# A hybrid decoder layer: mixer in source order, block inversion with one block per partition, TensorE output transposes, operands moved by 32 bytes

## The chip, the cores and the metric

The kernel runs on one core of one Trainium2 chip. The metric is the time of one execution in microseconds of device time; the smaller the better.

## What is computed

One decoder layer over 256 tokens of width 2048, all in float32: a SwiGLU feed-forward half step (FFN1), a mixer, a second feed-forward half step (FFN2), and a last RMSNorm. The mixer projects the normalised input with one weight `w_in` and feeds eight retention heads and eight gated DeltaNet heads; both join in one output projection `w_out`. The part that the change rewrites is the triangular solve of the DeltaNet heads.

```python
x = x + 0.5 * _swiglu(_rmsnorm(x, norm_ffn1_w), ffn1_w_gate, ffn1_w_up, ffn1_w_down)      # D_FF = 5632
x = x + _mixer(_rmsnorm(x, norm_mix_w), ...)
x = x + 0.5 * _swiglu(_rmsnorm(x, norm_ffn2_w), ffn2_w_gate, ffn2_w_up, ffn2_w_down)
# in _gated_delta, per head and chunk of the sequence:
m = where(strict, einsum(k_beta, k) * decay, 0.0);  a = m + eye
sol = triangular_solve(a, [v * beta, k_beta * exp(gc)], lower=True, unit_diagonal=True)
```

## The kernel before

Every large product is computed in three matmuls (`triple`, L149 to L151): weights and activations are split into a high and a low float32r part, and hi*hi, lo*hi and hi*lo are added up in PSUM. The activation tile (128x128: `xh`/`xl` for the normalised input, `hh`/`hl` for the hidden layer of an FFN, `mh`/`ml` and the like for the mixer's output) is the stationary operand, the weight (128x512) the moving one. A product of a 512-column block over 16 row tiles and two token tiles is 96 matmuls. The weights stream in as 512 KB pieces of two row tiles: SP issues the DMA into `raw` (four buffers), ScalarE makes `whi` (L135), VectorE `wlo` (L136), four buffers each; a piece is prepared three pieces before TensorE uses it. A piece feeds twelve matmuls.

The mixer runs 16 products with `w_in`, four for each of q, k, v and gate of both kinds of heads in two groups of four heads, then four with `w_out`. The small work of the heads is cut into generators in two lanes, `chains` and `side`. After each *unit* of a product (one `triple`, three matmuls) `advance` lets each lane go on until it says how many units to wait (`yield n`). That is the order of the source. In the FFNs the engines PE, DVE and Activation issue in that order (`tc.manual_schedule`); in the mixer before, the framework's scheduler orders all engines by its own estimate of times.

In `delta_chain` (L721) each group of four heads makes eight 128x128 unit triangular matrices `Nt`. Their inverse `Y` starts from the 32-row diagonal blocks (L795 to L829): the blocks are gathered in `Nd` by GpSimd, written to DRAM (`nd`), and spread by DMA from there so that each partition has the rows that it needs (`spread`, L806: four DMAs of 128 KB for every four columns j, eight times for each group, issued by GpSimd). For each of 31 columns VectorE makes one multiply and one subtract over 8 x (31-j) elements (L825, L826):

```python
V.tensor_tensor(yn[:, :, :w], nr[:, j - j0, :, j + 1:], Yd[:, :, j:j + 1].broadcast_to([P, NM, w]), ALU.mult)
V.tensor_tensor(Yd[:, :, j + 1:], Yd[:, :, j + 1:], yn[:, :, :w], ALU.subtract)
```

ScalarE and GpSimd copy the blocks into `Y` (L829), VectorE transposes them into `X` (L832), and two doubling levels of 64-column matmuls follow, four to a PSUM buffer (`quad`, L785, L791), each followed by a VectorE operation on the buffer. Seven calls of `four` (L709, L713; four matmuls of 128 columns) give the outputs. The DeltaNet and retention outputs are transposed on VectorE in 32x32 blocks (`vector_transposed`, L246, L254, into `mt`) and split into the stationary operands of `w_out` (`mixed_chain`, L919).

Where a tile lies: pools are stacked, and the pools of an FFN and `gd` of the mixer begin where the pools open at that time end. Worked out from the tiles' sizes (each padded to 32 bytes), `xh` and `xl` begin at an odd multiple of 32 bytes; `hh` and `hl` of FFN1 and the tiles of `gd` begin at a multiple of 64, since the pool `par` (2912 bytes) is open below them; for FFN2 `par` is closed, and `hh` and `hl` are back at an odd multiple of 32. The weight buffers are at an odd multiple of 32 all the time.

Of the kernel before, what the change touches and what calls it, by code (L numbers as in the profile page):

```python
# [31 lines left out]
LEAD = 3  # L32
NLEV = 7
# [3 lines left out]
JC = 4  # L37
# [14 lines left out]
C_EYE = C_SL + P  # L52
C_LEV = C_EYE + B0
# [5 lines left out]
def _constants():  # L59
# [12 lines left out]
    c[:, C_EYE:C_EYE + B0] = r % B0 == np.arange(B0)  # L72
# [15 lines left out]
def hybrid_layer(ctx: ExitStack, tc: tile.TileContext, a: dict, out: bass.AP):  # L88
# [10 lines left out]
    mx = ctx.enter_context(tc.tile_pool(name="mx", bufs=4, space=PSUM))  # L99
# [209 lines left out]
    def ffn(idx, factor, after, lead=None):  # L309
# [159 lines left out]
    with tc.tile_pool(name="gd", bufs=1) as gd:  # L469
        def mixed_out(o, b, xt=None):  # L470
            for t in range(NT):
# [4 lines left out]
        env = dict(x_left=x_left, ident=ident, mx=mx, product=product, product_units=product_units, power=power,  # L476
                   vector_transposed=vector_transposed, split=split,
# [34 lines left out]
def mixer(tc, a, gd, env):  # L512
    nc = tc.nc
    V, S, G, PE = nc.vector, nc.scalar, nc.gpsimd, nc.tensor
    x_left, ident, mx, power = (env[k] for k in ("x_left", "ident", "mx", "power"))
    vector_transposed, split = env["vector_transposed"], env["split"]
    product, product_units, weight_piece = (env[k] for k in ("product", "product_units", "weight_piece"))
# [6 lines left out]
    with ExitStack() as ctx:  # L524
# [61 lines left out]
        def gates_chain():  # L586
# [3 lines left out]
            yield 8  # L590
# [3 lines left out]
            weight_piece(src, KD, 2 * NH, both=(wab[:, :, 0, :], wab[:, :, 1, :]))  # L594
            abt = mx.tile([P, 512], F32, name="mx")
# [45 lines left out]
        def rotary_chain():  # L641
# [17 lines left out]
            for _ in range(2):  # L659
# [4 lines left out]
                for part in parts:  # L664
                    for tx in (th.bitcast(F32), tl):
                        V.scalar_tensor_tensor(ang, tx, -part, ang, ALU.mult, ALU.add)
# [5 lines left out]
            return  # L672
            yield
# [5 lines left out]
        def conv_chain(src, ct0, dst):  # L679

            y = pb.tile([P, GH, T], F32, name="y", bufs=1)
            for i in range(0, GH, 2):
# [11 lines left out]
                yield 2  # L694
            S.activation(dst, y, AF.Silu)
# [25 lines left out]
        def delta_chain(gi, kq, vT):  # L721

            hs = gi * GH
# [362 lines left out]
```

## Time and profile before

| | us |
|---|---|
| median of 3 runs (lowest, highest) | 2015.61 (2011.86, 2018.29) |
| the profiled execution | 2015.32 |
| its span, first to last instruction | 2013.5 |
| TensorE busy | 1974.1 (98%) |
| VectorE busy | 1315.8 (65%) |
| ScalarE busy | 890.9 (44%) |
| GpSimd busy | 86.9 (4%) |

The span is what the rows below divide up; the profiled execution is 1.8 us longer than its span. Busy time of TensorE counts modelled ends of pipelined matmuls, so it says that TensorE rarely waits, not that it runs at its peak. How fast it runs is read from the starts of its matmuls.

### The profile page before, as it was taken

How to read it: one execution, taken by the hardware profiler on the slowest of the kernel's cores; microseconds unless marked ns; L12 is line 12 of the kernel's file. 1: busy time of each engine (PE TensorE's matmuls, PEld its weight loads, DVE VectorE, ACT ScalarE, POOL GpSimd, SP SyncE). 2: the span in 40 equal slices, each digit the busy share in tenths (PEclk: the TensorE clock that was granted, in tenths of full speed). 3: DMA queues.
4: the chain of work that ended last, by engine and by line, in shares of the span. 5: the costliest groups of instructions: out<-in, count | busy, mean ns of one | idle time of the engine just before them, and what ended most of it. 6: DMA issues, size and time to landing. Idle time of an engine off the chain costs nothing.

```text
span 2013.5 us, 23688 instructions
## 1 busy us (share of the span) xinstructions
PE 1974.1 (98%) x8804; PEld 1617.5 (80%) x8804; DVE 1315.8 (65%) x1878; ACT 890.9 (44%) x1076; POOL 86.9 (4%) x121
## 2 busy tenths in 40 slices
PE   9999999999999999998998999999999999999998
PEld 7888888888888888866877778888888888888886
DVE  6776664457666766564896697766676554667654
ACT  6434443343444446633643344444444434444443
POOL 0000000000000000220132100000000000000000
PEclk9999999999999999998998999999999999999999
DMA  8655655565565566797468555666665556655564
GB/s 302 202 185 188 208 190 188 188 191 186 188 208 189 183 188 181 153 207 161 145 180 200 124 158 184 215 192 194 194 193 187 200 195 192 195 192 188 184 208 142
DMA packets 197604, 379.91 MB, mean 189 GB/s; under 512 B 15280, under 2 KB 15920, under 8 KB 197360
## 3 DMA queue, kind: packets, MB, share of 16 engines
q1 hardware_dynamic: 193888, 368.40, 59.5%
q0 software_dynamic: 3168, 8.65, 1.7%
q8 instruction: 69, 1.13, 0.2%
q10 hardware_dynamic: 432, 1.34, 0.2%
q14 instruction: 47, 0.39, 0.1%
HBM read 375.98 MB, written 2.36 MB: 188 GB/s over the span
## 4 chain that ended last, share of the span: by engine, by line
PE 85%; DVE 5%; DMA 4%; issue 4%; POOL 1%; ACT 1%; DVEq 0%; POOLq 0%; ACTq 0%
PE acc L149 28%; PE acc L151 27%; PE acc L150 27%; DMA nr<-nd 2%; DVE wlo L136 2%; DMA raw<-in_w_in_dram 1%; PE mx L791 1%; DVE mt L254 0%; PE mx L713 0%; DMA nd<-Nd 0%; DVE yn L825 0%; ACT whi L135 0%; DVE Yd L826 0%; POOL nr L810 0%; DVE ht L254 0%
## 5 line engine op out<-in xcount | busy, mean ns | idle before, releaser
L136 DVE TENSOR_TENSOR wlo<-raw,whi 128x1024 fp32r<-128x1024 f32 (+1 forms) x689 | 838.7, 1225 | 557.4 <-ACT whi L135 554.4
L135 ACT CAST whi<-raw 128x1024 fp32r<-128x1024 f32 (+1 forms) x689 | 719.3, 1050 | 859.4 <-PE acc L151 738.6
L149 PE MATMUL acc<-whi,xh 128*128 128x512 f32 x1920 | 760.5, 396 | 1.4 <-DVE xl L269 1.3
L150 PE MATMUL acc<-wlo,xh 128*128 128x512 f32 x1920 | 751.5, 391 | 6.7 <-DVE wlo L136 6.7
L151 PE MATMUL acc<-whi,xl 128*128 128x512 f32 x1920 | 750.8, 391 | 0.0
L150 PEld LDWEIGHTS acc<-wlo,xh 128*128 128x128 f32 x1920 | 362.1, 189 | 81.7 <-DVE wlo L136 10.8
L149 PEld LDWEIGHTS acc<-whi,xh 128*128 128x128 f32 x1920 | 362.1, 189 | 75.7 <-ACT whi L135 3.4
L151 PEld LDWEIGHTS acc<-whi,xl 128*128 128x128 f32 x1920 | 361.8, 188 | 75.4
L149 PE MATMUL acc<-whi,hh 128*128 128x512 f32 x704 | 276.5, 393 | 0.0
L150 PE MATMUL acc<-wlo,hh 128*128 128x512 f32 x704 | 276.5, 393 | 0.0
L151 PE MATMUL acc<-whi,hl 128*128 128x512 f32 x704 | 276.5, 393 | 0.0
L254 DVE STREAM_TRANSPOSE ht<-h 32x256 f32<-32x256 f32 x352 | 153.3, 436 | 5.3
L150 PEld LDWEIGHTS acc<-wlo,hh 128*128 128x128 f32 x704 | 132.4, 188 | 30.0
L151 PEld LDWEIGHTS acc<-whi,hl 128*128 128x128 f32 x704 | 132.4, 188 | 29.9
L149 PEld LDWEIGHTS acc<-whi,hh 128*128 128x128 f32 x704 | 132.4, 188 | 29.8
L141 ACT CAST hh<-ht 128x512 fp32r<-128x512 f32 x44 | 27.2, 618 | 121.3 <-DVE ht L254 121.3
L298 POOL TENSOR_TENSOR rfac<-rms,cexpn 128x2 f32<-128x2 f32 (+1 forms) x5 | 3.2, 642 | 866.0 <-DVE rms L304 866.0
L142 DVE TENSOR_TENSOR hl<-ht,hh 128x512 fp32r<-128x512 f32 x44 | 30.3, 688 | 14.5 <-ACT hh L141 14.4
L345 ACT ACTIVATE sg<-acc,rfac 128x512 f32<-128x512 f32 x44 | 29.9, 689 | 20.2 <-PE acc L151 17.4
L149 PE MATMUL acc<-whi,mh 128*128 128x512 f32 x96 | 38.1, 396 | 0.0
L151 PE MATMUL acc<-whi,ml 128*128 128x512 f32 x96 | 38.1, 396 | 0.0
L150 PE MATMUL acc<-wlo,mh 128*128 128x512 f32 x96 | 38.0, 396 | 0.0
(205 smaller groups left out, 843.8 us busy)
## 6 DMA issues: line engine op xcount, KB each, us to landing
raw<-in_ffn_w_up_dram SPq DMA_DIRECT2D x176, 512.0 KB, 4.4
raw<-in_ffn_w_down_dram SPq DMA_DIRECT2D x176, 512.0 KB, 4.4
raw<-in_ffn_w_gate_dram SPq DMA_DIRECT2D x175, 512.0 KB, 4.4
raw<-in_w_in_dram SPq DMA_DIRECT2D x128, 512.0 KB, 4.8
raw<-in_w_out_dram SPq DMA_DIRECT2D x32, 512.0 KB, 4.3
nr<-nd POOLq DMA_DIRECT2D x64, 128.0 KB, 7.7
x<-in_x_dram SPq DMA_DIRECT2D x4, 512.0 KB, 6.8
out_dram<-x SPq DMA_DIRECT2D x8, 256.0 KB, 2.4
```

The lines of the kernel that those rows point to most:

```text
L135: S.copy(hi, raw)
L136: V.tensor_tensor(lo, raw, hi.bitcast(F32), ALU.subtract)
L141: S.copy(hi, src)
L142: V.tensor_tensor(lo, src, hi.bitcast(F32), ALU.subtract)
L149: PE.matmul(o, lhsT=sh, rhs=hi, start=first, stop=False)
L150: PE.matmul(o, lhsT=sh, rhs=lo, start=False, stop=False)
L151: PE.matmul(o, lhsT=sl, rhs=hi, start=False, stop=last)
L254: V.transpose(dv[q:q + Q, :, :, r:r + Q], sv[r:r + Q, :, :, q:q + Q])
L298: G.tensor_tensor(dst, src, cexp[e][:, 0:1].broadcast_to([P, w]), ALU.pow)
L345: S.activation(sg[:, t, :], g[t], AF.Silu, scale=rf[:, t:t + 1])
L791: PE.matmul(pt[:m, i, :], lhsT=lhsT, rhs=rhs, start=True, stop=True)
```

## The change

- The mixer joins the FFNs: PE, DVE and Activation issue in source order (`tc.manual_schedule`), and the waits of the generators (`yield`) are set anew. Tiles are made late: `kq` and `vT` when the convolution needs them, a `pe` buffer (three now) only when the third last was read (`until`), `y` under a lock (`hold`), retention's `kT` and `v` when the group before is done. The query of retention's first group is projected earlier (in `mixer_plan` too); the rotary tables start with the first product.
- The blocks are inverted one per partition: 8 matrices x 4 blocks = 32 blocks, four copies of each (RS = 4), copy r holding the rows r, r+4, ... of the result. `nd` is written in 128-byte runs, loaded once as four DMAs of 128 KB (`Ub`); the recursion works on (31-j) x (j//4+1) elements; the result goes through DRAM a second time (`yd`, four DMAs, then `Yd`), in 128-byte runs. `spread` and its 64 DMAs are gone. `Y`'s copies are on ScalarE and VectorE.
- The quads have a PSUM pool of one buffer (`qd`), the other small work three (`mx`) in place of four.
- The outputs are transposed by TensorE through `mx`, and split from PSUM.
- A 32-byte tile `pad` is put first into FFN1's pool and into `gd`. With the constant `C_EYE` gone, `par` is 128 bytes smaller.

```diff
-    mx = ctx.enter_context(tc.tile_pool(name="mx", bufs=4, space=PSUM))
+    mx = ctx.enter_context(tc.tile_pool(name="mx", bufs=3, space=PSUM))
+    qd = ctx.enter_context(tc.tile_pool(name="qd", bufs=1, space=PSUM))
...
+            if idx == 1:
+
+                hp.tile([P, PAD], F32, name="pad")
...
-        for c0 in ([O_GK, O_GQ, O_GV, O_GZ, O_GZ + half] + [o + half for o in (O_GK, O_GQ, O_GV)]
-                   + [o + g for g in (0, half) for o in (O_RQ, O_RK, O_RV, O_RG)]):
+        for c0 in ([O_GK, O_GQ, O_GV, O_GZ, O_GZ + half, O_RQ] + [o + half for o in (O_GK, O_GQ, O_GV)]
+                   + [O_RK, O_RV, O_RG] + [o + half for o in (O_RQ, O_RK, O_RV, O_RG)]):
...
-    with tc.tile_pool(name="gd", bufs=1) as gd:
+    with tc.manual_schedule(engines={E.PE, E.DVE, E.Activation}), tc.tile_pool(name="gd", bufs=1) as gd:
+        gd.tile([P, PAD], F32, name="pad")
...
-        def finish_chains():
-            while chains or side:
+        def until(done):
+
+            while not done():
                 advance()
 
-        rf, gs = [], {}
+        held = set()
+
+        def hold(name):
+            while name in held:
+                yield 1
+            held.add(name)
+
+        rf, pes, read, PES = [], [], set(), 3
 
         def evacuated(col, dst=None, func=AF.Copy):
             ps, units = product_units(x_left, w_in, rows, col)
             run(units)
             if dst is None:
-                dst = pb.tile([P, NT, NB], F32, name="pe")
+
+                until(lambda: len(pes) < PES or id(pes[-PES]) in read)
+                dst = pb.tile([P, NT, NB], F32, name="pe", bufs=PES)
+                pes.append(dst)
             for t in range(NT):
                 S.activation(dst[:, t, :], ps[t], func, scale=rf[0][:, t:t + 1])
             return dst
...
         def conv_chain(src, ct0, dst):
+            yield from hold("y")
             y = pb.tile([P, GH, T], F32, name="y", bufs=1)
+            dst = dst()
...
-                yield 2
-            S.activation(dst, y, AF.Silu)
+                if i + 2 == GH:
+                    read.add(id(src))
+                    S.activation(dst, y, AF.Silu)
+                    held.discard("y")
+                yield 6
...
-            X = gd.tile([P, GH * NT, P], F32, name="X")
-            Y = gd.tile([P, GH * NT, P], F32, name="Y")
...
-                pt = mx.tile([P, 4, HALF], F32, name="mx")
+                pt = qd.tile([P, 4, HALF], F32, name="qd")
...
-            NM = GH * NT
+
+            NM, BS, RS = GH * NT, P // B0, P // (GH * NT * (P // B0))
+            BP = NM * BS
             Nd = gd.tile([P, NM, B0], F32, name="Nd", tag="st")
             for q in range(0, P, B0):
                 G.tensor_copy(Nd[q:q + B0], Ntf[q:q + B0, :, q:q + B0])
-            nd = dr.tile([P, NM * B0], F32, name="nd")
-            nc.gpsimd.dma_start(nd, Nd.rearrange("p m c -> p (m c)"))
-            ndv = nd.rearrange("(b j) x -> b (j x)", j=B0)
+            nd = dr.tile([NM, P, B0], F32, name="nd")
+            nc.gpsimd.dma_start(nd.rearrange("m p c -> p m c"), Nd)
+            Ub = gd.tile([P, B0, B0], F32, name="Ub", tag="X")
+            Yb = gd.tile([P, B0 // RS, B0], F32, name="Yb")
+            G.memset(Yb, 0.0)
+            for r in range(RS):
+                G.memset(Yb[r * BP:(r + 1) * BP].rearrange("p a c -> p (a c)")[:, r::B0 + RS], 1.0)
+            for r in range(RS):
+                nc.gpsimd.dma_start(Ub[r * BP:(r + 1) * BP].rearrange("p j c -> p (j c)"),
+                                    nd.rearrange("m (b j) c -> (m b) (j c)", j=B0))
+            Y = gd.tile([P, NM, P], F32, name="Y")
             G.memset(Y, 0.0)
-            Yd = gd.tile([P, NM, B0], F32, name="Yd")
-            G.tensor_copy(Yd, C(C_EYE, B0).unsqueeze(1).broadcast_to([P, NM, B0]))
-
-            def spread(j0):
-                nr = gd.tile([P, JC, NM, B0], F32, name="nr", bufs=2)
-                n = JC * NM * B0
-                for b in range(P // B0):
-                    nc.gpsimd.dma_start(nr[b * B0:(b + 1) * B0].rearrange("p j m c -> p (j m c)"),
-                                        ndv[b, j0 * NM * B0:j0 * NM * B0 + n].partition_broadcast(B0))
-                return nr
-
-
-            yield 4
-            nrs = [spread(0)]
-            yield 14
-            for j0 in range(0, B0, JC):
-                if j0 + JC < B0:
-                    nrs.append(spread(j0 + JC))
-                nr = nrs[j0 // JC]
-                for j in range(j0, min(j0 + JC, B0 - 1)):
-                    w = B0 - 1 - j
-                    yn = gd.tile([P, NM, B0], F32, name="yn")
-                    V.tensor_tensor(yn[:, :, :w], nr[:, j - j0, :, j + 1:], Yd[:, :, j:j + 1].broadcast_to([P, NM, w]), ALU.mult)
-                    V.tensor_tensor(Yd[:, :, j + 1:], Yd[:, :, j + 1:], yn[:, :, :w], ALU.subtract)
-                    yield 2
+
+
+            yield 28
+            for j in range(B0 - 1):
+                w, n = B0 - 1 - j, j // RS + 1
+                yn = gd.tile([P, 3 * B0], F32, name="yn")
+                yv = yn[:, :n * w].rearrange("p (i c) -> p i c", c=w)
+                V.tensor_tensor(yv, Ub[:, j:j + 1, j + 1:].broadcast_to([P, n, w]), Yb[:, :n, j:j + 1].broadcast_to([P, n, w]), ALU.mult)
+                V.tensor_tensor(Yb[:, :n, j + 1:], Yb[:, :n, j + 1:], yv, ALU.subtract)
+                yield 1
+            yd = dr.tile([NM, P, B0], F32, name="yd")
+            for r in range(RS):
+                nc.gpsimd.dma_start(yd.rearrange("m (b a r) c -> r (m b) a c", b=BS, r=RS)[r], Yb[r * BP:(r + 1) * BP])
+            Yd = gd.tile([P, NM, B0], F32, name="Yd", tag="st")
+            nc.gpsimd.dma_start(Yd, yd.rearrange("m p c -> p m c"))
+            yield 32
             for i, q in enumerate(range(0, P, B0)):
-                (S.copy, G.tensor_copy)[i % 2](Y[q:q + B0, :, q:q + B0], Yd[q:q + B0])
-            yield 10
+                (S.copy, V.tensor_copy)[i % 2](Y[q:q + B0, :, q:q + B0], Yd[q:q + B0])
+            yield 2
+            X = gd.tile([P, NM, P], F32, name="X")
...
+            def kq(part):
+                if part == 0:
+                    ins["kq"] = gd.tile([P, GH, 2, T], F32, name="kq")
+                return ins["kq"][:, :, part, :]
+
+            def vT():
+                ins["vT"] = gd.tile([P, GH, T], F32, name="vT", tag="ml")
+                return ins["vT"]
+
+            chains.append(conv_chain(evacuated(O_GK + cs), 8 + hs, partial(kq, 0)))
+            chains.append(conv_chain(evacuated(O_GQ + cs), hs, partial(kq, 1)))
+            chains.append(conv_chain(evacuated(O_GV + cs), 16 + hs, vT))
+            chains.append(delta_chain(gi, ins))
...
-            mt = gd.tile([P, GH, T], F32, name="mt", tag="dec")
-            for piece in vector_transposed(mt, src):
-                yield 2
-                piece()
             for i in range(0, GH, 2):
-                yield 1
-                split(parts[0][:, i:i + 2], parts[1][:, i:i + 2], mt[:, i:i + 2])
+                yield 3
+                pt = mx.tile([P, 2, T], F32, name="mx")
+                for j in range(2):
+                    for t in range(NT):
+                        PE.transpose(pt[:, j, t * P:(t + 1) * P], src[:, t, (i + j) * P:(i + j + 1) * P], ident)
+                split(parts[0][:, i:i + 2], parts[1][:, i:i + 2], pt)
+            read.add(id(src))
...
         def rotated_chain(src, dst):
...
-            yield 6
+            read.add(id(src))
+            yield 8
             for t in range(NT):
                 V.tensor_tensor(r[:, t, :, 0, :], r[:, t, :, 0, :], t2[:, t, :, 0, :], ALU.subtract)
                 V.tensor_tensor(r[:, t, :, 1, :], r[:, t, :, 1, :], t2[:, t, :, 1, :], ALU.add)
-            yield 5
+            yield 6
...
+        def rotated(col, name):
+            src = evacuated(col)
+            dst = rt.tile([P, GH, T], F32, name=name)
+            side.append(rotated_chain(src, dst))
+            return dst
+
+        def retention_products(gi, qT):
             hs, cs = gi * GH, gi * GW
-            q = evacuated(O_RQ + cs)
-            qT = rt.tile([P, GH, T], F32, name="rqT")
-            side.append(rotated_chain(q, qT))
-            k = evacuated(O_RK + cs)
-            kT = rt.tile([P, GH, T], F32, name="rkT")
-            side.append(rotated_chain(k, kT))
+            kT = rotated(O_RK + cs, "rkT")
+            until(lambda: len(done) == gi)
...
+        done = []
         chains.append(gates_chain())
+        side.append(rotary_chain())
         delta_products(0)
         delta_gate(0)
         delta_gate(1)
-        side.append(rotary_chain())
+        q0 = rotated(O_RQ, "rqT")
         delta_products(1)
-        r0 = retention_products(0)
+        r0 = retention_products(0, q0)
         chains.append(mixed_chain(NH, gates[0], ["kq"]))
         chains.append(mixed_chain(NH + GH, gates[1], ["X", "Y"]))
         chains.append(mixed_chain(0, r0, ["At", "Nt"]))
-        r1 = retention_products(1)
+        r1 = retention_products(1, rotated(O_RQ + GW, "rqT"))
...
-        finish_chains()
+        until(lambda: not chains and not side)
```

## Rows read from the trace of the kernel before

**Rows 1.** One line of the code: FFN1's gate activations, 4 blocks of 2 products.

```profile
L345 ACT ACTIVATE sg<-acc,rfac x8: 689/690/691, 117.4 to 248.6; 128x512 f32<-128x512 f32 x8
```

**Rows 2.** First and last matmul starts of the w_in stage, in TensorE's timeline.

```profile
735.20 0.39 PE L149 MATMUL acc<-whi,xh 128*128 128x512 f32 x1
...
1195.48 0.39 PE L149 MATMUL acc<-whi,m 128*128 128x512 f32 x1
```

**Rows 3.** Same timeline: small matmuls between two units (start, length).

```profile
937.89 0.33 PE L791 MATMUL mx<-X,Nt 128*128 128x64 f32 x2
...
938.81 0.33 PE L791 MATMUL mx<-X,Nt 128*128 128x64 f32 x2
...
822.14 0.60 PE L701 MATMUL mx<-ident,kq 128*128 128x128 f32 x4
...
823.97 0.60 PE L701 MATMUL mx<-ident,kq 128*128 128x128 f32 x4
...
955.10 1.05 PE L713 MATMUL mx<-vh,Y 128*128 128x128 f32 x8
...
957.37 1.05 PE L713 MATMUL mx<-w,kd 128*128 128x128 f32 x8
```

**Rows 4.** Stretches: busy us of each engine (instructions), granted clock, DMA share, GB/s.

```profile
730.00:1210.00 480.00, 453.92 (x2157) 369.51 (x2156) 334.87 (x644) 222.00 (x322) 84.16 (x113) 0.98 0.68 169
...
860.00:870.00 10.00, 8.02 (x28) 6.55 (x29) 9.65 (x19) 3.36 (x4) 1.93 (x4) 0.83 0.63 136
910.00:920.00 10.00, 2.97 (x11) 2.25 (x10) 5.66 (x11) 3.94 (x5) 1.18 (x3) 0.66 1.03 186
...
1090.00:1100.00 10.00, 6.01 (x22) 5.34 (x22) 5.22 (x11) 2.11 (x4) 1.65 (x2) 0.53 0.65 136
```

**Rows 5.** Waits of the w_in stage: who for whom, us, times, longest.

```profile
DVE yn L825 <- DMA nr<-nd: 24.9, 6, 9.2
...
PE mx L791 <- DVE X L832: 13.0, 2, 7.0
```

**Rows 6.** Weight DMAs at 740 to 750, then 895 to 910: KB, us to landing.

```profile
raw<-in_w_in_dram SPq DMA_DIRECT2D x4, 512.0 KB, 4.2
...
raw<-in_w_in_dram SPq DMA_DIRECT2D x4, 512.0 KB, 10.8
```

**Rows 7.** DMA issues of nd and of one narrow weight, then nr's range.

```profile
nd<-Nd POOLq DMA_DIRECT2D x2, 128.0 KB, 4.5
raw<-in_w_in_dram SPq DMA_DIRECT2D x1, 128.0 KB, 5.2
...
DMA to landing us min/median/max: 3.7/7.7/10.7
```

**Rows 8.** One line: additions after four down products, FFN1, then FFN2.

```profile
L365 DVE SCALAR_TENSOR_TENSOR x<-acc,x x8: 679/682/684, 303.5 to 405.3; 128x512 f32<-128x512 f32 x8
...
L365 DVE SCALAR_TENSOR_TENSOR x<-acc,x x8: 681/682/684, 1579.8 to 1678.4; 128x512 f32<-128x512 f32 x8
```

**Rows 9.** Stretches inside the w_out products and FFN2's down products.

```profile
1200.00:1250.00 50.00, 50.00 (x215) 40.22 (x214) 37.78 (x54) 22.35 (x30) 0.00 (x0) 1.00 0.57 194
1600.00:1650.00 50.00, 50.00 (x223) 41.39 (x222) 25.03 (x23) 19.42 (x19) 0.00 (x0) 1.00 0.57 195
```

**Rows 10.** VectorE's timeline at the first recursion: idle time before, in brackets.

```profile
859.92 0.42 DVE L825 TENSOR_TENSOR yn<-nr,Yd 128x248 f32<-128x248 f32 x1 [9.15 <-DMA nr<-nd]
```

**Rows 11.** TensorE's timeline just after it.

```profile
861.98 0.80 PE L150 MATMUL acc<-wlo,xh 128*128 128x512 f32 x1 [2.45 <-DVE wlo L136]
```

**Rows 12.** Lines of the stage by form: busy us, mean ns, idle before.

```profile
L136 DVE TENSOR_TENSOR wlo<-raw,whi 128x1024 fp32r<-128x1024 f32 x143 | 176.2, 1236 | 62.9 <-ACT whi L135 62.2
...
L254 DVE STREAM_TRANSPOSE mt<-pe 32x256 f32<-32x256 f32 x32 | 14.0, 436 | 0.6
...
L843 DVE TENSOR_TENSOR Pm<-mx,cst 128x256 f32<-128x256 f32 x8 | 3.4, 425 | 19.6 <-PE mx L791 19.6
...
L825 DVE TENSOR_TENSOR yn<-nr,Yd 128x40 f32<-128x40 f32 x2 | 0.4, 204 | 0.1
```

More of the change, by code (lines that the diff above doesn't have):

```diff
@@ L32 @@
 LEAD = 3
+PAD = 8
 NLEV = 7
@@ L36 @@
 B0 = 1 << LEV0
-JC = 4
 RET_W = NH * HD
@@ L51 @@
 C_SL = C_U + P
-C_EYE = C_SL + P
-C_LEV = C_EYE + B0
+C_LEV = C_SL + P
 C_INVF = C_LEV + (NLEV - LEV0) * HALF
@@ L474, in mixed_out @@
             later.extend(norm_block(ssqs[2], 2, b, xt))
-        env = dict(x_left=x_left, ident=ident, mx=mx, product=product, product_units=product_units, power=power,
-                   vector_transposed=vector_transposed, split=split,
+        env = dict(x_left=x_left, ident=ident, mx=mx, qd=qd, product=product, product_units=product_units, power=power,
+                   split=split,
                    weight_piece=weight_piece, do_later=do_later, mixed_out=mixed_out,
@@ L514, in mixer @@
     V, S, G, PE = nc.vector, nc.scalar, nc.gpsimd, nc.tensor
-    x_left, ident, mx, power = (env[k] for k in ("x_left", "ident", "mx", "power"))
-    vector_transposed, split = env["vector_transposed"], env["split"]
-    product, product_units, weight_piece = (env[k] for k in ("product", "product_units", "weight_piece"))
+    x_left, ident, mx, qd, power = (env[k] for k in ("x_left", "ident", "mx", "qd", "power"))
+    product, product_units, weight_piece, split = (env[k] for k in ("product", "product_units", "weight_piece", "split"))
     w_in = a["w_in"][0]
@@ L664, in rotary_chain @@
                 for part in parts:
+                    yield 4
                     for tx in (th.bitcast(F32), tl):
@@ L671, in rotary_chain @@
             S.activation(cosT, ang, AF.Sin)
-            return
-            yield
         def bc(ap, n=P):
@@ L719, in mixer, with delta_chain @@
         gates, mixed = {}, []
-        def delta_chain(gi, kq, vT):
+        def delta_chain(gi, ins):
             hs = gi * GH
+            kq, vT = ins["kq"], ins["vT"]
             kT, qT = kq[:, :, 0, :], kq[:, :, 1, :]
@@ L908, in delta_products @@
             hs, cs = gi * GH, gi * GW
-            k = evacuated(O_GK + cs)
-            kq = gd.tile([P, GH, 2, T], F32, name="kq")
-            chains.append(conv_chain(k, 8 + hs, kq[:, :, 0, :]))
-            q = evacuated(O_GQ + cs)
-            chains.append(conv_chain(q, hs, kq[:, :, 1, :]))
-            v = evacuated(O_GV + cs)
-            vT = gd.tile([P, GH, T], F32, name="vT", tag="ml")
-            chains.append(conv_chain(v, 16 + hs, vT))
-            chains.append(delta_chain(gi, kq, vT))
+            ins = {}
+            def kq(part):
[9 more added lines that the diff above has]
+            chains.append(delta_chain(gi, ins))
         def mixed_chain(r0, src, tags):
@@ L929, in mixed_chain @@
             mixed.append((r0, *parts))
-            mt = gd.tile([P, GH, T], F32, name="mt", tag="dec")
-            for piece in vector_transposed(mt, src):
-                yield 2
-                piece()
             for i in range(0, GH, 2):
-                yield 1
-                split(parts[0][:, i:i + 2], parts[1][:, i:i + 2], mt[:, i:i + 2])
+                yield 3
[5 more added lines that the diff above has]
+            read.add(id(src))
         def rotated_chain(src, dst):
+            yield from hold("y")
             r = pb.tile([P, NT, GH, 2, 64], F32, name="y", bufs=1)
@@ L948, in rotated_chain @@
                 V.tensor_tensor(r[:, t], sv[:, t], cb, ALU.mult)
-            yield 6
+            read.add(id(src))
+            yield 8
             for t in range(NT):
@@ L960, in rotated_chain @@
                 S.copy(dst[:, i:i + 2, :], pt)
+                if i + 2 == GH:
+                    held.discard("y")
                 yield 1
@@ L989, in retention_chain @@
                 S.copy(o[:, t], op[t])
+            done.append(hs)
             yield 3
@@ L1013, in retention_chain @@
             gate.append(None)
-        def retention_products(gi):
-            hs, cs = gi * GH, gi * GW
-            q = evacuated(O_RQ + cs)
-            qT = rt.tile([P, GH, T], F32, name="rqT")
-            side.append(rotated_chain(q, qT))
-            k = evacuated(O_RK + cs)
-            kT = rt.tile([P, GH, T], F32, name="rkT")
-            side.append(rotated_chain(k, kT))
+        def rotated(col, name):
[4 more added lines that the diff above has]
+        def retention_products(gi, qT):
+            hs, cs = gi * GH, gi * GW
+            kT = rotated(O_RK + cs, "rkT")
+            until(lambda: len(done) == gi)
             v = evacuated(O_RV + cs, rt.tile([P, NT, NB], F32, name="rv"))
```

2 lines of the change are left out of this document (removed).

## The prediction

> **What bounds the kernel now.** I read the windows first, then the starts of the large matmuls, then the waits and the DMA rows inside the mixer. Four blocks of FFN1 put their first and last gate activations at 117.4 and 248.6 us [rows 1]; less the 0.7 us by which the second of a pair follows the first, six products took 130.5 us, so a product of 96 matmuls takes 21.75 us and a matmul 226.6 ns, with nothing in between. In the FFNs TensorE is the bound and has no gaps to give. Its rate, however, is not the same everywhere. The additions that close FFN1's four down products span 101.8 us, those of FFN2's 98.6 us [rows 8], for the same 432 matmuls between them: 3.2 us, or 7.4 ns for each. In w_out 50 us hold 215 matmuls, in FFN2's down product 223, both at a granted clock of 1.00 [rows 9]: the mixer's output operands run at the slower rate too.
>
> The mixer is the place that loses time. Its 16 w_in products go from 735.20 to 1195.48 us [rows 2]: 460.3 us, against 16 x 21.75 = 348.0. The excess is 112.3 us. Part of it is the heads' own work on TensorE, which stays. A unit of three large matmuls with one quad matmul takes 0.92 us instead of 0.68: 0.24 each. Two units with four transposes take 1.83 instead of 1.36: 0.47. Two units with a `four` take 2.27: 0.91 for 512 columns [rows 3]. From the code there are 64 quad matmuls (15.4 us), 32 sets of transposes (15.0), 14 `four` (12.7), and 8 x 512 + 8 x 384 + 2 x 1536 columns in decay products, scores and retention outputs (about 18 at the same price per column). The gates' product and the cumulated decays I estimate at 7. Together 68. The other 44 us are waits, and lost clock.
>
> Where are they? The whole stretch has 480 - 453.9 = 26.1 us of idle TensorE; three stretches of 10 us hold 13.0 of it (2.0, 7.0 and 4.0), and in just these the granted clock falls to 0.83, 0.66 and 0.53 [rows 4], which means a third, two thirds and nearly all of them at 1.2 GHz instead of 2.4. Each fall comes with TensorE having stood idle for microseconds. Half of the busy time at the low level is lost: 1.7 + 1.5 + 2.8 = 6 us. All three lie where `spread` runs. VectorE waits 24.9 us for `nr`, and TensorE 13.0 us, in two waits, for `X`, that is for the end of the recursion [rows 5]. The `nr` transfers also slow the weights: a 512 KB piece lands in 10.8 us there, in 4.2 before the recursion [rows 6]. A piece is used up in 12 x 0.2266 = 2.72 us, so three pieces of lead are 8.2 us, and 10.8 is too late. I put 5 us of short weight waits to this: 13 + 6 + 5 = 24 of the 44 us belong to `spread`. The other 20 are spread over hand-offs between TensorE and VectorE.
>
> **The change, part by part.**
>
> *The 32 bytes.* FFN1's `hh`/`hl` and the tiles of `gd` move to an odd multiple of 32 bytes, where `xh` and FFN2's `hh` lie already, which run at 226.6 ns. 2 x (4 x 144 + 4 x 120)/2 = 1056 matmuls of FFN1's down products and 384 of w_out gain 7.4 ns each: 7.8 + 2.8 = 10.6 us. All of them are on the path, as nothing interrupts them. The bounds are 0 (the address is not the cause) and 10.6. I take 10.6: address is all that differs between the two FFNs' down products.
> [...]
>
> *`spread` goes.* 64 DMAs of 128 KB become, in each group, one of 128 KB out (`nd`), four in (`Ub`), four quarter-size ones out (`yd`) and one in (`Yd`). The steady interference has no source any more: -24 us. What takes its place are two trips to DRAM, each awaited once. First trip: GpSimd's four gathers, its memsets and the issues of the DMAs, for which I estimate 6 us; `nd`, 4.5 us; a landing of `Ub` at `nr`'s median 7.7 [rows 7]: 18 us, against 28 units x 0.68 = 19.0 us of cover. With both landings at `nr`'s longest, 10.7, it is 27 us and VectorE stands 8 us too long. Its price is known: before, VectorE stood 9.15 us [rows 10] and TensorE then 2.45 [rows 11], so some 6.7 us are free. Second trip: 3 us of issues by estimate, 7.7 and 4.5, 15 us, or 24 with two landings of 10.7, against 32 units = 21.8 us. I take 0 for both trips, with 0 to 16 us as bounds, 16 being what the same hand-off cost before: 13 us of waiting for `X` and 3 of clock.
> The 128-byte runs are new. A row near it: the narrow weight piece, 128 KB in runs of 64 bytes, landed in 5.2 us, `nd` in runs of 1 KB in 4.5 [rows 7]. So I let short runs cost nothing more.
> The Trainium skill (DMA: Bandwidth & Descriptors, Specifications) asks for 512 bytes at least, below which the engines read, modify and write; by that rule the trips would be the third case below. The row of the 64-byte runs does not show it.
>
> *The recursion on VectorE.* An operation of 248 elements takes 0.42 us, one of 40 takes 0.204 [rows 10, 12], or 0.16 + 1.02 ns per element. The elements fall from 3968 to 1560 in 31 pairs: 18.2 us become 13.3 for each group. The 64 transposes into `mt` go, at 0.436: 28 us. VectorE is not on the path, so both are worth only the cover they add. In the 31 units of a recursion, 21 us, VectorE now has 13.3 + 8 x 1.24 for splits [rows 12] = 23 us to do; the 6.7 us above take up the 2.
>
> *Transposes on TensorE.* 16 x 2 = 32 transposes, 8 sets of 0.47 [rows 3]: +3.8 us, on the path.
>
> *Source order, and fewer buffers.* Every engine now stands at the head of its own queue. The second group's quads end in the second unit of a weight piece, behind a split of 1.24 us on VectorE (I counted the yields); the single quad buffer then keeps TensorE waiting some 0.5 us for each of eight quads: 4 us. The first group's end at the last unit of a piece, ahead of the next split, and cost nothing. Three `mx` buffers under six sets of transposes in a row at the end of the mixer, where seven steps have no product under them, and the norm factors that VectorE awaits from GpSimd, I keep at the old price. VectorE is less full there: of the 20 us of hand-offs I drop 8. Left are 20 - 8 + 4 = 16 us; the bounds are 4 (every hand-off covered) and 53 (below). Earlier rotary tables and late-made tiles move work into products with free VectorE time: 0. Where that cover is gone, one split late is 1.2 us.
>
> **Sum,** against the profiled execution of 2015.3 us, which is 0.3 below the median of the three runs: 2015.3 - 10.6 - 44 + 16 + 3.8 = 1980.5. I predict 1980 us.
>
> **The rivals.**
>
> *Few waits are left.* The hand-offs shrink to 4 us. For it: the first recursion's products lose only a split here and there. Against it: the old kernel, with four buffers, did not get there. 1980 - 12 = 1968.
>
> *The trips are late.* The wait for `nr` turns into one for `Ub` and `Yd`: 16 us again, 1996. For it: in-order VectorE blocks the splits behind it, and 27 us is more than 19. Against it: only an eighth of the bytes is loaded.
>
> *The shift does nothing.* Then the two rates come from something else that differs between FFN1 and FFN2: 1980 + 10.6 = 1991. Against it stands the w_out stretch, which shares only the address with FFN1.
>
> *In-order queues become the bound (slower).* TensorE, in source order, reaches each of 16 quads and 14 `four` results while VectorE still has a whole split and the operation itself ahead: 1.24 + 0.43 = 1.67 us [rows 12], or 1.9 with the longer operation behind a `four`. 16 x 1.67 + 14 x 1.9 = 53 us, of which 4 are counted: 2029. It decides from 35 / 30 = 1.2 us per hand-off. For it: there is one quad buffer where there were four. Against it: the first group's quads end ahead of the split.
>
> **How the numbers follow.** The forecast (1971 to 1987) has 0.50; few waits (1964 to 1971) 0.21; late trips (1987 to 2000) 0.13; a shift without effect 0.06; the slower case 0.05; the same queues at half that price, about no change, 0.02; still faster than 1964, 0.03. The range 1965 to 2000 leaves out about 0.12. A change below 0.3%, 6 us, can't be told from none: faster 0.93, same 0.02, slower 0.05.
>
> **What would show it.** The FFN1 down products should take 98.6 us where they took 101.8, and w_out 223 matmuls in 50 us. The w_in stage should fall from 460 to some 436 us, with granted clock 1.00 in nearly all of it and weights landing in 4 to 5 us throughout. VectorE's waits for `nr` should be replaced by a wait for `Ub` under 6 us; TensorE's waits for `X` should be gone, and small waits for `Pm` or `Y` in the second group should be there. The prediction is wrong if `Ub` or `Yd` land more than 25 us after their source, if the address changes no rate, or if TensorE's idle time in the mixer stays above 25 us.

## The result, and the profile after

The changed kernel takes 2026.11 us (median of 4 runs, 2025.33 to 2027.28), the kernel before 2015.92 in the same comparison: a ratio of 1.0053, 95% interval 1.0036 to 1.0071. It is slower by half a per cent, where 1980 us and 1.8% faster were forecast. The profiled execution took 2025.3 us, with a span of 2023.6 where it was 2013.5.

Outside the mixer's first stage the large matmuls reached the expected rate. The additions behind FFN1's four down products now span 98.5 us, as FFN2's do [rows 8], and a stretch of 50 us in w_out holds 222 matmuls where it held 215 [rows 9]:

```profile
L367 DVE SCALAR_TENSOR_TENSOR x<-acc,x x8: 680/682/684, 302.8 to 401.3; 128x512 f32<-128x512 f32 x8
```

The stretches of the changed kernel (busy us of PE, PEld, DVE, ACT, POOL with their instructions, granted clock, DMA share, GB/s):

```profile
727.00:1200.00 473.00, 439.96 (x2100) 355.92 (x2098) 306.58 (x609) 211.17 (x311) 57.00 (x71) 0.97 0.62 150
770.00:780.00 10.00, 7.55 (x26) 5.57 (x24) 5.90 (x10) 6.63 (x8) 0.00 (x0) 0.83 0.32 90
...
820.00:830.00 10.00, 7.75 (x25) 5.95 (x26) 6.89 (x19) 4.17 (x5) 2.58 (x2) 0.66 0.66 129
860.00:960.00 100.00, 98.25 (x479) 79.35 (x478) 62.32 (x118) 40.13 (x45) 9.47 (x16) 1.00 0.81 169
1000.00:1010.00 10.00, 3.95 (x14) 2.42 (x14) 7.76 (x14) 3.98 (x6) 0.00 (x0) 0.89 0.51 158
1010.00:1020.00 10.00, 3.23 (x7) 2.35 (x8) 7.60 (x16) 5.19 (x7) 4.79 (x5) 0.50 0.20 56
1215.00:1265.00 50.00, 50.00 (x222) 41.42 (x221) 32.10 (x42) 21.17 (x27) 0.00 (x0) 1.00 0.55 179
```

The 100 us of the first recursion, 860 to 960, are nearly full and at full clock; there the old kernel had two of its three low-clock stretches [rows 4]. But the w_in stage as a whole grew from 460.3 us [rows 2] to 472.6, between these two matmuls of TensorE's timeline:

```profile
727.39 0.39 PE L148 MATMUL acc<-whi,xh 128*128 128x512 f32 x1
...
1199.95 0.47 PE L148 MATMUL acc<-whi,m 128*128 128x512 f32 x1
```

The holes are elsewhere now: 1000 to 1020 us is two thirds empty, and the clock falls to 0.50 in it. TensorE's idle time from 727 to 1200 us is 33.0 us (473.00 - 439.96), above the 25 that the prediction named as a sign of being wrong. The waits of TensorE and ScalarE from 727 to 1300 us (engine, line, waited for: us, times, longest) name the places:

```profile
PE mx L754 <- DVE gu L750: 16.5, 2, 11.5
PE acc L149 <- DVE wlo L135: 7.3, 7, 1.5
PE mx L987 <- DVE y L980: 4.0, 4, 2.1
PE qd L808 <- DVE Pm L862: 3.1, 2, 2.4
PE acc L148 <- ACT whi L134: 2.4, 2, 1.7
...
ACT y L705 <- DVE y L707: 31.3, 12, 3.6
```

TensorE's wait for `X` [rows 5] is gone but for 0.2 us, and VectorE waits for no DMA of the inversion. In its place TensorE stands 16.5 us, in two waits, at the decay products (L754), and ScalarE stands twelve times in the convolution (L705). One stretch of the three engines' timelines shows both (start, length, instruction, and in brackets the idle time before it with what ended it), ScalarE first, then VectorE, then TensorE:

```profile
994.52 0.47 ACT L705 ACTIVATE y<-mx,cw 128x256 f32<-128x256 f32 x1 [3.03 <-DVE y L707]
996.64 1.06 ACT L711 ACTIVATE kq<-y 128x1024 f32<-128x1024 f32 x1 [1.65 <-DVE y L707]
997.61 1.03 ACT L134 CAST whi<-raw 128x1024 fp32r<-128x1024 f32 x1
...
995.03 1.52 DVE L707 SCALAR_TENSOR_TENSOR y<-mx,cw,y 128x255 f32<-128x255 f32 x3 [0.54 <-ACT y L705]
998.67 1.23 DVE L135 TENSOR_TENSOR wlo<-raw,whi 128x1024 fp32r<-128x1024 f32 x1 [2.12 <-ACT whi L134]
...
1015.76 1.65 DVE L750 TENSOR_SCALAR gu<-cst,g 128x128 fp32r<-128x128 f32 x8
...
1004.90 0.40 PE L150 MATMUL acc<-whi,xl 128*128 128x512 f32 x1
1016.77 1.49 PE L754 MATMUL mx<-gu,slr 128*128 128x512 f32 x2 [11.47 <-DVE gu L750]
```

ScalarE waits 3.03 us for VectorE's part of the convolution; the high split (`whi`) stands behind that; VectorE then waits 2.12 us for the split. So the two engines work in turn, weights are prepared late, and when TensorE reaches the decay product at 1005 us, VectorE needs 11 us more to come to that place in its list.

### The profile page after: what moved, and what is told of

Same layout as the page of the kernel before. It is cut to its first block, busy times and chain, and to the rows that moved or that the text cites. A ratio compares the mean times of both kernels' runs of the same rounds, so it can differ in the third digit from the quotient of the medians.

```text
span 2023.6 us, 23594 instructions
## 1 busy us (share of the span) xinstructions
PE 1972.1 (97%) x8836; PEld 1620.1 (80%) x8836; DVE 1289.1 (64%) x1818; ACT 888.5 (44%) x1074; POOL 59.7 (3%) x79
## 4 chain that ended last, share of the span: by engine, by line
PE 86%; DVE 8%; ACT 3%; issue 2%; DMA 1%; ACTq 0%; POOLq 0%; DVEq 0%
PE acc L148 28%; PE acc L149 27%; PE acc L150 27%; DVE wlo L135 3%; ACT whi L134 2%; DVE y L707 1%; PE qd L808 1%; DMA raw<-in_w_in_dram 1%; DVE y L253 1%; PE mx L731 1%; DVE yn L837 1%; DVE Yb L838 0%; PE mx L791 0%; DVE sq L253 0%; DVE ht L253 0%
## 5 line engine op out<-in xcount | busy, mean ns | idle before, releaser
L707 DVE SCALAR_TENSOR_TENSOR y<-mx,cw,y 128x255 f32<-128x255 f32 (+2 forms) x72 | 34.6, 481 | 8.2 <-ACT y L705 6.5
```

The source lines that it names most:

```text
L707: V.scalar_tensor_tensor(yy[:, lag:], pt[:, j, :T - lag], w[:, 3 - lag:4 - lag], yy[:, lag:], ALU.mult, ALU.add)
```

## The experiments

Twelve kernels were run, each beside the kernel before on the same chip, so ratios are to that kernel. The median of the kernel before lies between 2015.9 and 2017.4 us in the five comparisons, so a difference in us between two kernels of different comparisons is good to some 1.5 us. After the result the theory was: the time is lost by the order of ScalarE's and VectorE's instructions in the convolution; the rivals: VectorE's total load, or another part of the change. The short diffs are against the changed kernel or the kernel before, as said.

**The multiplies first** (changed kernel, `conv_chain`).

```diff
                 for j in range(2):
+                    S.mul(y[:, i + j, :], pt[:, j, :], cw[:, ct0 + i + j, 3:4])
+                for j in range(2):
                     w = cw[:, ct0 + i + j, :]
                     yy = y[:, i + j, :]
-                    S.mul(yy, pt[:, j, :], w[:, 3:4])
```

> The changed kernel, with one edit in the convolution: both multiplies of ScalarE come ahead of VectorE's six operations, where the source has multiply, three operations, multiply, three operations. The theory: in source order ScalarE's second multiply waits for VectorE's first three operations (47 us of such waits after, 4.5 before), the next high splits queue behind it and the low splits behind those, the lead of three weight pieces is used up, and TensorE stands at the decay products behind late VectorE work. Then the waits of ScalarE for VectorE at the convolution fall under 5 us, the stops of TensorE near 772, 817 and 990 to 1017 us shrink, and the time is 1990 to 2002 us (25 to 35 less than the changed kernel's 2026). The rival: VectorE's whole load in its fixed order is what TensorE waits for, whatever order the multiplies have; then the time is above 2018.

Measured: 2019.46 us, ratio 1.0012 (1.0003 to 1.0022); 6.7 us less than the changed kernel. The theory's 1990 to 2002 us is missed, and the time lies in the rival's range. The waits at L705 are gone, but ScalarE now stands at the SiLU that ends a convolution, and TensorE at the decay products nearly as long:

```profile
PE mx L755 <- DVE gu L751: 14.9, 3, 10.8
...
ACT kq L712 <- DVE y L708: 14.3, 3, 6.0
ACT vT L712 <- DVE y L708: 9.0, 2, 6.0
```

The wait had moved one instruction on. Hence the two runs below in which the SiLU stands later.

**The 32 bytes alone, then 160** (kernel before; `PAD` = 8 or 40 floats).

```diff
+            if idx == 1:
+                hp.tile([P, PAD], F32, name="pad")
             hh = hp.tile([P, len(halves[0]) * kb, T], F32R, name="hh")
...
     with tc.tile_pool(name="gd", bufs=1) as gd:
+        gd.tile([P, PAD], F32, name="pad")
```

> The kernel before with the two 32-byte tiles alone. If the address of the stationary operand sets the rate, FFN1's down products and w_out run at 226.6 ns for each matmul and the time is 2005 us, 10.6 less than before, the w_in stage keeping its 460 us. If the rates came from something else in the change, the time stays at 2015.9.

Measured: ratio 0.9989 (0.9980 to 0.9998), some 2 us. Neither. FFN1's down additions span 101.0 us, between the 101.8 and 98.6 of [rows 8]:

```profile
L369 DVE SCALAR_TENSOR_TENSOR x<-acc,x x8: 680/682/684, 303.9 to 404.9; 128x512 f32<-128x512 f32 x8
```

So an odd multiple of 32 is not what matters. The changed kernel's operands lie another 128 bytes lower, since its constants are smaller.

> The kernel before with two tiles of 160 bytes in place of the 32. With 32 bytes alone the operands began at 32 modulo 256 and a matmul took 232.4 ns; in the changed kernel, where the constants are 128 bytes smaller too, they begin at 160 modulo 256 and it took 226.7. If the address modulo 256 sets the rate, FFN1's down products and w_out run at 226.7 here and the time is 2005 to 2007 us, the w_in stage keeping its 460 us; if something else in the changed kernel made the rate, 232 to 234 ns and 2013 to 2016 us.

Measured: 2006.79 us, ratio 0.9953 (0.9938 to 0.9968), and 98.6 us between the additions (304.3 to 402.9). As expected: the 10.6 us of the sum are about right, the 32 bytes as their reason are not.

**The weights moved by 128 bytes** (kernel before, one tile of 128 bytes ahead of the pool of the split weights).

> The kernel before with 128 bytes ahead of the split weights, so that they begin at 32 modulo 256 instead of 160; the normalised input stays at 160, the hidden layer of FFN1 and the mixer's outputs come to 128, that of FFN2 to 32. If the rate follows from the distance between the two operands (0: 226.7 ns, 128: 232.4, 96: 234.3, as the runs so far have it), gates, ups and w_in run at 232.4 ns, FFN1's down and w_out at 234.3, FFN2's down at 226.7. If it follows from the stationary operand's address alone (160: 226.7, 32: 232.4), gates, ups and w_in keep 226.7 and FFN2's down runs at 232.4.

Measured: one run, 2041.78 us. The three lines are FFN1's gate activations of the last three blocks, FFN1's down additions and FFN2's:

```profile
L347 ACT ACTIVATE sg<-acc,rfac x6: 687/688/689, 523.1 to 613.0; 128x512 f32<-128x512 f32 x6
...
L367 DVE SCALAR_TENSOR_TENSOR x<-acc,x x8: 678/682/684, 310.4 to 412.2; 128x512 f32<-128x512 f32 x8
...
L367 DVE SCALAR_TENSOR_TENSOR x<-acc,x x8: 678/680/683, 1600.8 to 1699.3; 128x512 f32<-128x512 f32 x8
```

(89.9 - 0.7) / 384 = 232.3 ns for the gates and ups, 101.8 us and 98.5 us for the down products: the distance theory in all three. The normalised input did not move and lost its fast rate.

**The scheduler back** (changed kernel, the mixer without `tc.manual_schedule`).

```diff
-    with tc.manual_schedule(engines={E.PE, E.DVE, E.Activation}), tc.tile_pool(name="gd", bufs=1) as gd:
+    with tc.tile_pool(name="gd", bufs=1) as gd:
```

> The changed kernel with the mixer left to the framework's scheduler again; inversion, waits of the generators, buffers, transposes and the 32 bytes are kept. If the fixed order of the engines' queues is what costs (the convolution's alternation or any other), the w_in stage falls under 440 us and the time is 1975 to 1992 us. If the loss lies in the single quad buffer, the late tiles, the trips through DRAM or the transposes on TensorE, the time stays above 2015 us.

Measured: 1999.79 us, ratio 0.9916 (0.9899 to 0.9933); 26.3 us less than the changed kernel, though 8 above the range expected of a fixed order that costs. It does cost; but the w_in stage takes 453 us, since VectorE now waits for the inversion's DMAs and TensorE for the splits behind them:

```profile
PE acc L148 <- ACT whi L134: 9.0, 2, 6.5
PE acc L149 <- DVE wlo L135: 4.7, 4, 1.9
...
DVE Y L847 <- DMA Yd<-yd: 16.2, 2, 10.4
DVE yn L837 <- DMA Ub<-nd: 6.0, 2, 4.1
ACT y L705 <- DVE y L707: 3.2, 4, 1.2
```

**The inversion alone** (kernel before with the new lines from `NM, BS, RS` to the copies into `Y`).

> The kernel before with the new inversion alone (one block per partition, two trips through DRAM, no repeated loads), the generators' waits of the inversion with it; scheduler, four small buffers and VectorE's transposes as before. If the repeated loads cost what the prediction put to them, the time is 1986 to 1994 us (24 to 30 less than before), the clock is 1.00 through the first recursion and weights land in 4 to 5 us there. If the trips through DRAM are late or something else starves TensorE there, the time is above 2005 us.

Measured: 2006.52 us, ratio 0.9951 (0.9936 to 0.9966): 10.1 us, a third to two fifths of what was put to the repeated loads, and just above 2005. TensorE's 13.0 us for `X` [rows 5] are gone, but late low splits rose from 5.0 to 14.4, and the clock still falls, to 0.66 from 900 to 910 us, where 1.00 was expected:

```profile
PE acc L150 <- DVE wlo L136: 14.4, 6, 6.1
...
DVE Y L827 <- DMA Yd<-yd: 19.4, 2, 10.6
DVE yn L817 <- DMA Ub<-nd: 12.2, 2, 9.2
```

VectorE stands 31.6 us for the two trips where it stood 24.9 for `nr`.

**The trips given more time** (the scheduler version, `yield 28` to 34 and `yield 32` to 40).

> The changed kernel with the framework's scheduler (1999.8 us), and the two trips through DRAM given 34 and 40 units instead of 28 and 32. In the run before, the scheduler let VectorE stand 16 us for the second trip and 6 us for the first, with late splits behind. If the units set where the recursion and the copies stand in the order, these waits fall under 8 us and the time is 1988 to 1996 us. If the scheduler places them by its own estimate of the transfers, the waits stay and the time is 1997 to 2004 us.

Measured: 2008.20 us, ratio 0.9957 (0.9945 to 0.9970), slower than without the edit and above both expected ranges. VectorE's waits stay, 15.4 and 12.2 us: under the scheduler the units of the source don't place the copies. The longer chain also left quads, outputs and mixed transposes with no product under them at the end of the stage: 13 us between two large matmuls.

**The SiLU later, alone and with the multiplies first** (changed kernel).

```diff
                 if i + 2 == GH:
                     read.add(id(src))
+                    yield 4
                     S.activation(dst, y, AF.Silu)
                     held.discard("y")
-                yield 6
+                    yield 2
+                else:
+                    yield 6
```

> The changed kernel with one edit: the SiLU that ends each convolution stands four units after VectorE's last operation on the tile, where the changed kernel has it directly behind. The run with the multiplies first showed ScalarE standing 4.7 to 6.0 us at each such SiLU, with the next high split behind it, and VectorE then 2.1 to 3.3 us for that split; TensorE still stood 10.8 us at the decay products. Theory: the SiLU at the head of ScalarE's queue is the larger part of the alternation; alone, its move gives 8 to 15 us, 2011 to 2018 us, since the second multiply still waits. Rival: VectorE simply has 9.4 us of work in the 12 units of a convolution (8.2 us and some 1.9 of transposes), and no order of ScalarE helps: 2023 to 2029.

Measured: 2018.42 us, 7.7 less than the changed kernel (ratio 1.0010, 1.0001 to 1.0019) and 0.4 above the expected 2011 to 2018. ScalarE's waits at L705 stay, at 30.1 us.

> The changed kernel with both edits, the multiplies first and the SiLU four units later. Theory: ScalarE waits for VectorE nowhere in a convolution, the lead of three pieces holds through the three convolutions in a row, the stops at the decay products (6.5 and 12.9 us after) shrink to under 3 us together, and the time is 1995 to 2005 us. Rival, VectorE's load: within 4 us of the run with the multiplies first, 2015 to 2020.

Measured: 2008.81 us, ratio 0.9966 (0.9952 to 0.9980). Together they give 17.3 us, where 6.7 and 7.7 make 14.4; by the ratios to the kernel before it is 17.5 against 8.3 and 8.7. So the two add up within the noise. But 2009 is above the expected 2005, and ScalarE still stands 16.1 us at the SiLUs, where the theory had it stand nowhere. TensorE still waits 8.9 us for the decay products' operands, behind a VectorE that is full in three convolutions in a row: from 967.8 to 996.6 us its timeline has two waits, of 0.93 us each. The last 10 us of it (idle time stands in brackets):

```profile
988.02 2.94 DVE L708 SCALAR_TENSOR_TENSOR y<-mx,cw,y 128x255 f32<-128x255 f32 x6 [0.93 <-ACT y L703]
990.88 2.90 DVE L135 TENSOR_TENSOR wlo<-raw,whi 128x1024 fp32r<-128x1024 f32 x2
993.70 2.92 DVE L708 SCALAR_TENSOR_TENSOR y<-mx,cw,y 128x255 f32<-128x255 f32 x6
996.54 1.22 DVE L135 TENSOR_TENSOR wlo<-raw,whi 128x1024 fp32r<-128x1024 f32 x1
```

So the rival of VectorE's load has its share.

**More cover at every hand-off, order kept.** To both edits this adds `yield 7` instead of 6 between convolution steps, 4 instead of 2 ahead of the decay products, 10 instead of 6 ahead of the rotated transposes, two halves of one bank for the quads, four `pe` buffers, and `yield 20` for 28 in the inversion.

> The version with both edits of the convolution (2008.8 us), source order kept, and more room at each hand-off at which TensorE still stood: convolution steps 7 units apart instead of 6, decay products 4 units behind VectorE's part instead of 2, the transposes of the rotated query and key 10 instead of 6, two halves of a bank for the quads in turn instead of one buffer, four pe buffers so that the last mixed transposes have a product under them; the first wait of the inversion is 20 units instead of 28, so that the chain ends where it did. If the loss left is in-order hand-offs with too little cover, the stops at the decay products (3.9 and 7.4 us), at the rotated transposes (2.3 and 4.5), at the quads (2.8 and 1.1) and at the mixed transposes (3.7) fall to a third and the time is 1985 to 1996 us. If VectorE is full there whatever the spacing, the stops move to other lines and the time is 2003 to 2012 us.

Measured: 2003.68 us, ratio 0.9944 (0.9928 to 0.9959): 5.1 us better, at the other theory's end. The decay products' wait fell from 8.9 to 3.7 us and the rotated transposes' from 4.8 to 1.3, but the quads' rose from 3.3 to 8.0, and w_out's late splits stayed.

**The cover that was still lacking** (on top of the last):

```diff
-                yield 4
+                yield 6
                 dp = mx.tile([P, 4, P], F32, name="mx")
...
                 for i in range(4):
-                    yield 1
+                    if i % 2 == 0:
+                        yield 1
...
-                yield 2
+                yield 4
                 for sl, Xl in zip(quads, left):
...
                     V.tensor_tensor(pms[-1], d, msk, ALU.mult)
+                yield 4
...
-            o = product(m_left, a["w_out"][0], OUT_ORDER, b * NB)
+            o = product(m_left, a["w_out"][0], OUT_ORDER, b * NB, step=3)
```

`step` is the number of units between two pieces of the norm that runs under w_out (2 before).

> The spaced version in source order (2003.7 us) with the hand-offs that its trace still shows: quad matmuls two to a unit so that four units stand between VectorE's transposes or masks and the quads that read them (its waits there: 1.4, 1.0, 1.3, 2.0 and 1.6 us), decay products six units behind VectorE's part instead of four (2.6 us), and in w_out the pieces of the next norm every third unit instead of every second (late splits of 1.5 us each, and 1.3 us at FFN2's first transposes). If cover is what lacks, 1991 to 1998 us; if VectorE's load moves the stops elsewhere, 2000 to 2006 us.

Measured: 1994.23 us, ratio 0.9887 (0.9871 to 0.9904), within the expected range; 31.9 us less than the changed kernel, with the mixer still in source order. The w_in stage is 446.5 us, w_out and the start of FFN2 have no late split left. What stays in the w_in stage is mostly the quads:

```profile
PE qd L817 <- DVE Pm L871: 7.1, 2, 4.7
PE mx L758 <- DVE gu L754: 2.6, 4, 1.3
PE acc L149 <- DVE wlo L135: 1.7, 3, 0.9
```

**Inversion and 160 bytes together** (kernel before, nothing else).

> The kernel before with the new inversion and the 160-byte tiles, and nothing else of the change: scheduler, four small buffers and VectorE's transposes as before. The inversion alone gave 10.1 us and the 160 bytes 9.3. If the two parts act in different places (FFN1 and w_out on one side, the w_in stage on the other), they add up: 1996 to 1999 us. If the faster operands use up cover that the inversion needs, 2000 to 2005 us.

Measured: 1996.99 us, ratio 0.9902 (0.9887 to 0.9917). They add up. Both this and the last spaced version beat both kernels, and they lie 2.8 us apart: two parts of the change, with the scheduler kept, come close to what source order reached after its waits had been set twice more.

## Why the prediction was wrong

The runs give the change as a sum of differences of medians: 2015.9 - 9.3 (operands' address) - 10.1 (inversion, under the scheduler) + 3.3 (the rest of the change under the scheduler, as what is left to 1999.8) + 26.3 (source order) = 2026.1.

**The step that failed is "Source order, and fewer buffers".** It counted 16 us of hand-offs: 4 for the second group's quads, and 12 of the old 20. The stage's waits in the trace after sum to 32.8 us: 16.5 at the decay products, 4.4 for low splits (of the 7.3 above, the rest lies in w_out), 4.0 at the rotated transposes, 3.3 at the quads, 2.4 for high splits and 2.2 smaller ones. The low clock costs 9.7 more: in the stretches where the granted clock was at its lower level, 0.50 or 1.2 GHz, TensorE was busy for 19.5 us, and half of that is lost. In the kernel before it was busy for 16.0 us in such stretches, a loss of 8.0; the prediction had 6, because its slices of 10 us left out the ends of two of the falls. The sums over these stretches, before (862.0 to 865.4, 913.2 to 923.4, 1090.7 to 1100.9 us) and after (775.8 to 779.2, 820.1 to 826.9, 1007.9 to 1021.6, 1110.3 to 1113.7, 1130.7 to 1134.1 us):

```profile
sum 23.80, PE 16.03 PEld 13.76 DVE 12.71 ACT 5.60 POOL 2.94; mean PE 5.34 PEld 4.59 DVE 4.24 ACT 1.87 POOL 0.98
...
sum 30.70, PE 19.49 PEld 14.82 DVE 21.00 ACT 12.63 POOL 6.42; mean PE 3.90 PEld 2.96 DVE 4.20 ACT 2.53 POOL 1.28
```

So 42.5 us stand against 16. The quads (3.3 for 4) and the other hand-offs (13.0 for 12) are close to the forecast. What the step lacked are the decay products, which it did not mention, with 16.5 us, and the clock, with 9.7. It took "Every engine now stands at the head of its own queue" and looked mainly at TensorE behind VectorE. What decides is the order between ScalarE and VectorE: late-made tiles were put at 0, as work that moves into "products with free VectorE time", and the convolution was not priced at all. In the old trace ScalarE waits in the convolution's multiplies twice, for 2.5 us in all; in the new one twelve times, for 31.3:

```profile
ACT y L690 <- DVE y L692: 2.5, 2, 2.0
```

The convolution's order gives back 17.3 of the 26.3 us. The 31.3 us are a sign and not the price: in the last spaced version ScalarE still stands 16.9 us at the SiLUs (10.0 + 4.8 + 2.1).

The Trainium skill (PSUM — Partial Sum Buffer, Engine vs sequencer instructions) states that the queues of ScalarE, VectorE and GpSimd are strictly first in, first out. The trace agrees: with 3.03 us of ScalarE waiting at 994 us, the split behind it did not pass.

**"The other 20 are spread over hand-offs": the 44 us were a remainder, and too large.** The excess of 112.3 us less an estimated 68 of the heads' own work was called waiting. The wait view of the kernel before, summed over the same stage, says less; beside the 13.0 of [rows 5] it has

```profile
PE acc L150 <- DVE wlo L136: 5.0, 5, 2.5
PE mx L983 <- DVE sc L975: 3.3, 3, 2.2
PE mx L772 <- DVE vh L763: 2.8, 1, 2.8
PE mx L713 <- DVE w L876: 1.3, 1, 1.3
PE mx L735 <- DVE gu L731: 0.4, 1, 0.4
```

25.8 us with the 13.0; with 8.0 for the clock 33.8. So the heads' own work is about 78 us and not 68, and only 34 us were there to gain. After, the excess is 472.6 - 348.0 = 124.6 us, and 124.6 - 32.8 - 9.7 = 82.1 is the 78 plus the 3.8 for TensorE's transposes. Against the forecast 436 us of the stage the 36.6 too many are 26.5 of waits and clock above 16 and 10.2 that were never waits. Which term of the 68 was too small is not shown.

**W_out was left out of the sum.** It, with FFN2's first products, takes 8.8 us that the sum doesn't have: 3.0 above 21.75 us in its first product (0.9 of them two sets of the transposes already priced), 4.0 in its last, and 1.8 more at FFN2's start. In the fixed order eight transposes of the next norm stand ahead of a low split there (VectorE, then TensorE):

```profile
1286.41 3.59 DVE L253 STREAM_TRANSPOSE y<-x 32x256 f32<-32x256 f32 x8
1290.03 1.23 DVE L135 TENSOR_TENSOR wlo<-raw,whi 128x1024 fp32r<-128x1024 f32 x1
...
1291.31 0.50 PE L149 MATMUL acc<-wlo,mh 128*128 128x512 f32 x1 [1.51 <-DVE wlo L135]
```

With four of them between splits the last spaced version has no such wait. With the stage's 36.6 us these 8.8 are, within 1 us, the whole distance from 1980.5 to the profiled execution.

**`spread`** was right in kind. Its waits are gone, and 860 to 960 us is at full clock. Its 24 us can't be confirmed as one number: in source order its places improved while others got worse, and under the scheduler only 10.1 came out. That the two trips cost nothing is true of the changed kernel (no DMA wait of VectorE) and false under the scheduler: there the rival of late trips happened. Short runs cost nothing in `nd`: written in runs of 128 bytes it landed in 4.1 us, in runs of 1 KB before in 4.5 [rows 7]. The recursion's operations take 27.9 us for both groups, against 2 x 13.3 forecast. Weights land in 8.2 us (median) from 890 to 920 us, not in the 4 to 5 claimed; since `nr` is gone there, it is not shown that its transfers were what slowed them before.

**The 32 bytes**: the size was right, 10.9 us in the trace of the changed kernel (8.0 in FFN1, 2.9 in w_out), the reason was not. Alone they give 2.

**The rivals.** The one that ended slower said 2029 and was 3 us off the time, with a chance of 0.05. Its mechanism, 30 hand-offs of quads and outputs each behind a whole split, is not what happened, so that its time came near is luck. It had the right place to look, the fixed queues, and the wrong pair of engines.

What stays open: how the 9.0 us that the source order costs beyond the convolution split among the rotated transposes, the end of the mixer and w_out; the two spaced versions moved several waits at once.

## What to carry to other kernels

When a scheduled stage is put into source order, read every pair of engines that alternate on one tile, not only those that feed the bound; here two engines that each waited for the other starved the third, though all were idle part of the time. A remainder (excess less estimated work) should be checked against the sum of the trace's waits before it is called gain. Two parts of the change paid by themselves, the inversion with 10.1 us and the operands' address with 9.3; and with units re-spaced where the trace showed stops, the mixer in source order ran 1.1% faster than the kernel before.

## What was not expected of the hardware

The rate of a 128x512 matmul depends in these runs on where its two operands lie relative to each other. As the mean distance between the starts of such matmuls in the traces, it takes 226.7 ns with both at the same offset modulo 256 bytes (w_in before, FFN1's down products after), 232.4 with the two 128 bytes apart (the 32 bytes alone), and 234.3 with the stationary operand at 0 and the weight at 160 (FFN1's down products before). Moving the weights by 128 bytes slowed the products whose stationary operand had not moved, and left alone those whose two operands moved together. Other distances were not tried, and why the distance matters is not shown.
The Trainium skill (TensorE: Matmul & The Clock Gate, Back-to-back issue gap) gives 216 ns for an isolated matmul of 512 columns and about 131 ns for one in a stream, and has no term for the operands' address there; the runs show three rates, all above both.
